# A 3x3 convolution with residual: one image at a time on the full 128x128 array, with row pairs packed on chip

## The chip, the cores and the metric

The kernel runs on one core of one Trainium2 chip. The metric is the device time of one execution in microseconds (us): the median of several executions. Before the change it is 126.52 us, the median of 8 runs between 126.23 and 126.70.

A core has a matrix engine (TensorE, PE in the profile), a vector engine (VectorE, DVE), a scalar engine (ScalarE, ACT), GpSimd (POOL) and SyncE (SP). PE reads SBUF and writes PSUM; the others compute from SBUF and PSUM or only issue transfers. Transfers between HBM and SBUF run on 16 DMA engines, fed by queues which SP, ACT and POOL issue into.

## The reference

`x` and `residual` are 16 x 64 x 64 x 64 in fp32 (images, channels, rows, columns), `weight` is 64 x 64 x 3 x 3. With zero padding of one pixel:

```python
for kh in range(k):
    for kw in range(k):
        output[b, co] += weight[co, ci, kh, kw] * x_pad[b, ci, kh:kh+h, kw:kw+w]
return (output + residual).astype(np.float32)
```

for all images b, output channels co and input channels ci. `x`, `residual` and the output are 16.78 MB each.

## The kernel before

**Tiling.** Two images make a pair: 2 x 64 channels fill the 128 partitions, with one image's 4,096 pixels along each partition. There are 8 pairs. Every pair has its own buffer for x (`xt`, bf16) and its own for the residual (`ro`, fp32), so no load waits for a buffer.

**Loads.** ACT issues the load of the weights (L52). POOL issues the eight x loads (L54), 2 MB each in HBM, cast to bf16 by the DMA; between the first and the rest it makes an identity matrix. SP issues the eight residual loads (L58), 2 MB each. SP also issues the stores (L106), after all residual loads.

**Weights.** VectorE duplicates the weights (L61), PE transposes the nine taps (L67), and VectorE casts the result into `wl` (L70): on partitions 0 to 63 and again on 64 to 127, nine 64 x 64 matrices.

**Convolution.** For a pair, the loop at L79 goes over four chunks of 2 x 8 rows. A chunk has two PSUM tiles of one bank (512 columns). Each of nine taps takes four matmuls of K = 64, M = 64 (L91), one for each 64 x 64 quarter of the array: two images (`half`) times two groups of rows (`swap`). In the second PSUM tile the two images stand exchanged, so that all four quarters are in use. Each matmul has its own weight load. A pair takes 4 x 9 x 4 = 144 matmuls, the kernel 1,152.

**Adding and storing.** VectorE adds the first PSUM tile to the residual in place with one instruction over 128 partitions (L100), and the second with two over 64 partitions each (L105). When a pair's four chunks are done, SP stores it (L106).

**Order.** The loops are written out in full, each engine takes its instructions from the tile framework's schedule, and the framework puts in all waits. [...] up to four chunks can be in work.

Of the kernel before, what the change touches and what calls it, by code (L numbers as in the profile page):

```python
# [1 line left out]

# [5 lines left out]

FP32 = mybir.dt.float32
BF16 = mybir.dt.bfloat16  # L10
ADD = mybir.AluOpType.add


@with_exitstack
def kernel(
    ctx: ExitStack,
    tc: tile.TileContext,
    x: bass.AP,
    weight: bass.AP,
    residual: bass.AP,  # L20
    out: bass.AP,
):
    nc = tc.nc

    B, C, H, W = x.shape
    CO = weight.shape[0]
    K = weight.shape[2]
    assert C == 64 and CO == 64 and K == 3 and H == 64 and W == 64 and B == 16

    NPIX = H * W  # L30
    NPAIR = B // 2
    ROWS = 8
    CHUNK = ROWS * W
    NCHUNK = NPIX // CHUNK

    TAPS = [(1, 1), (1, 0), (1, 2), (0, 1), (0, 0), (0, 2), (2, 1), (2, 0), (2, 2)]

    res_bc = residual.rearrange("b c h w -> (b c) (h w)")
    out_bc = out.rearrange("b c h w -> (b c) (h w)")
    x_bc = x.rearrange("b c h w -> (b c) (h w)")  # L40
    w_flat = weight.rearrange("co ci kh kw -> co (ci kh kw)")

    pool = ctx.enter_context(tc.tile_pool(name="pool", bufs=1))
    psum = ctx.enter_context(tc.tile_pool(name="psum", bufs=8, space=bass.MemoryType.PSUM))


    wdup = pool.tile([64, 2, 576], FP32)
    ident = pool.tile([64, 64], FP32)
    ro = [pool.tile([128, NPIX], FP32, name=f"ro{p}") for p in range(NPAIR)]
    xt = [pool.tile([128, NPIX], BF16, name=f"xt{p}") for p in range(NPAIR)]  # L50

    nc.scalar.dma_start(out=wdup[:, 0, :], in_=w_flat[:, :])  # L52
    for p in range(NPAIR):
        nc.gpsimd.dma_start(out=xt[p][:, :], in_=x_bc[128 * p : 128 * p + 128, :])  # L54
        if p == 0:
            make_identity(nc, ident[:, :])
    for p in range(NPAIR):
        nc.sync.dma_start(out=ro[p][:, :], in_=res_bc[128 * p : 128 * p + 128, :])  # L58


    nc.vector.tensor_copy(out=wdup[:, 1, :], in_=wdup[:, 0, :])  # L61
    wl = pool.tile([128, 9, 64], BF16)
    wdup3 = wdup.rearrange("p d (ci t) -> p (d ci) t", t=9)
    for t0, n in ((0, 8), (8, 1)):
        tp = psum.tile([128, CHUNK], FP32, name="ps")
        for t in range(t0, t0 + n):
            nc.tensor.transpose(  # L67
                out=tp[:, 64 * (t - t0) : 64 * (t - t0) + 64], in_=wdup3[:, :, t], identity=ident[:, :]
            )
        nc.vector.tensor_copy(  # L70
            out=wl[:, t0 : t0 + n, :], in_=tp[:, 0 : 64 * n].rearrange("p (t c) -> p t c", c=64)
        )

    for p in range(NPAIR):
        x3 = xt[p].rearrange("p (h w) -> p h w", w=W)
        o = ro[p]
        for c in range(0, NCHUNK, 2):  # L79
            ps = [psum.tile([128, CHUNK], FP32, name="ps") for _ in range(2)]  # L80
            ps3 = [t.rearrange("p (h w) -> p h w", w=W) for t in ps]
            for i, (kh, kw) in enumerate(TAPS):
                xlo, xhi = max(0, 1 - kw), min(W, W + 1 - kw)
                for swap in range(2):
                    r0 = ROWS * (c + swap)
                    ylo = max(0, 1 - kh - r0)
                    yhi = min(ROWS, H + 1 - kh - r0)
                    for half in range(2):
                        hp = slice(64 * half, 64 * half + 64)
                        to = 64 * (half ^ swap)  # L90
                        nc.tensor.matmul(  # L91
                            out=ps3[swap][to : to + 64, ylo:yhi, xlo:xhi],
                            lhsT=wl[hp, 3 * kh + kw, :],
                            rhs=x3[hp, r0 + ylo + kh - 1 : r0 + yhi + kh - 1, xlo + kw - 1 : xhi + kw - 1],
                            start=i == 0,
                            stop=i == len(TAPS) - 1,
                            skip_group_check=True,
                        )
            sl = slice(CHUNK * c, CHUNK * (c + 1))
            nc.vector.tensor_tensor(out=o[:, sl], in0=ps[0][:, :], in1=o[:, sl], op=ADD)  # L100
            sl = slice(CHUNK * (c + 1), CHUNK * (c + 2))
            for half in range(2):
                hp = slice(64 * half, 64 * half + 64)
                fr = 64 - 64 * half
                nc.vector.tensor_tensor(out=o[hp, sl], in0=ps[1][fr : fr + 64, :], in1=o[hp, sl], op=ADD)  # L105
        nc.sync.dma_start(out=out_bc[128 * p : 128 * p + 128, :], in_=o[:, :])  # L106


# [1 line left out]
_INS = ['x', 'weight', 'residual']  # L110
_OUTS = [((16, 64, 64, 64), 'float32')]


# [23 lines left out]
```

## Time and profile before

| | before |
|---|---|
| median of 8 runs | 126.52 us |
| the profiled execution | 126.68 us |
| its span, first to last instruction | 124.9 us |
| PE busy, matmuls | 66.5 us (53%), 1,161 |
| VectorE busy, instructions | 67.5 us (54%), 99 |
| ACT busy | 0 |
| moved by DMA | 404 GB/s over the span |
| add over 128 x 512 (L100), mean | 692 ns, x32 |
| add over 64 x 512 (L105), mean | 688 ns, x64 |
| copy of the weights (L61), 64 x 576 fp32 | 453 ns |

The span is what the profile can see; the execution's time has 1.8 us more around it. A PE that is shown as busy is not necessarily at its peak, since matmuls overlap: a single one is shown as 384 ns long, [...]. Durations come from one profiled execution, and the other runs lie within 0.2% of the median.

In the page's picture of the span in 40 slices, DMA stands at 9 tenths or more from slice 2 to slice 38, and PE and VectorE are at work from slice 4 to slice 31.

### The profile page before, as it was taken

To read this page: it belongs to the slowest core of one execution; us is meant where nothing else is said; L and a number is where in the kernel's file an instruction comes from. 1 tells how busy PE (TensorE), PEld (TensorE's weight loads), DVE (VectorE), ACT (ScalarE), POOL (GpSimd) and SP (SyncE) were. 2 spreads that over 40 slices of the span, in tenths; PEclk is the share of its full clock that TensorE was granted. 3 is DMA by queue.
4 is the path that set the end of the run, shared out by engine and by line. 5 is a ranking of instruction groups with operands and counts; after the bars stand their busy time and mean duration, and the time that the engine had idled before them with its cause. 6 is when DMAs were issued, how large, how long until landed. Compare 5 with 4: busy or idle time off the path is not lost.

```text
span 124.9 us, 2518 instructions
## 1 busy us (share of the span) xinstructions
PE 66.5 (53%) x1161; PEld 55.3 (44%) x1161; DVE 67.5 (54%) x99; POOL 4.9 (4%) x14
## 2 busy tenths in 40 slices
PE   0003079979949949949967976985990000000000
PEld 0003049948928928927946954963980000000000
DVE  0001204998996996995995995997898000000000
POOL 6900000000000000000000000000000000000000
PEclk9999999999999999999999999999998555555555
DMA  4999999999999999999999999999999999999970
GB/s 100 370 328 299 352 310 296 338 333 299 304 341 315 315 344 307 328 336 296 302 336 331 307 336 333 304 317 420 425 430 420 451 430 425 430 420 436 430 325 10
DMA packets 3547, 42.25 MB, mean 338 GB/s; under 512 B 401, under 2 KB 401, under 8 KB 465
## 3 DMA queue, kind: packets, MB, share of 16 engines
q1 hardware_dynamic: 2304, 33.56, 64.2%
q0 software_dynamic: 1152, 8.39, 32.1%
q8 instruction: 9, 0.15, 0.4%
q10 hardware_dynamic: 80, 0.15, 0.3%
q14 instruction: 2, 0.01, 0.0%
HBM read 33.70 MB, written 16.78 MB: 404 GB/s over the span
## 4 chain that ended last, share of the span: by engine, by line
DMA 35%; PE 27%; DVE 6%; another core or an unknown queue 6%; POOL 1%; issue 1%; DVEq 1%; POOLq 0%
DMA xt<-in_x_dram 35%; PE ps L91 27%; DVE ro L105 4%; DVE ro L100 2%; POOL xt L54 1%; DVEq L132 1%; POOL ident masks.py:199 0%; POOL ident masks.py:197 0%; POOLq masks.py:199 0%; POOLq L121 0%
## 5 line engine op out<-in xcount | busy, mean ns | idle before, releaser
L91 PE MATMUL ps<-xt,wl 64*64 64x504 bf16 (+3 forms) x1152 | 65.2, 384 | 15.8 <-DMA xt<-in_x_dram 15.8
L91 PEld LDWEIGHTS <-wl 64*64 64x64 bf16 x1152 | 54.2, 110 | 26.5 <-DMA xt<-in_x_dram 15.1
L105 DVE TENSOR_TENSOR ro<-ps,ro 64x512 f32<-64x512 f32 x64 | 44.1, 688 | 1.3
L100 DVE TENSOR_TENSOR ro<-ps,ro 128x512 f32<-128x512 f32 x32 | 22.1, 692 | 15.3 <-PE ps L91 14.6
L67 PE MATMUL ps<-ident,wdup 64*128 64x64 f32 x9 | 1.3, 320 | 11.5 <-DVE wdup L61 11.5
L61 DVE COPY wdup<-wdup 64x576 f32<-64x576 f32 x1 | 0.5, 453 | 10.9 <-DMA wdup<-in_weight_dram 10.9
L67 PEld LDWEIGHTS ps<-ident,wdup 64*128 64x128 f32 x9 | 1.1, 205 | 11.5 <-issue 11.5
L54 POOL DMA_DIRECT2D xt<-in_x_dram x8 | 4.4, 583 | 0.8 <-POOLq L121 0.8
L70 DVE CAST wl<-ps 128x512 bf16<-128x512 f32 (+1 forms) x2 | 0.8, 454 | 1.3 <-PE ps L67 1.3
masks.py:199 POOL TENSOR_SCALAR_AFFINE_SELECT ident<-ident 64x64 f32<-64x64 f32 x1 | 0.3, 271 | 0.1
masks.py:197 POOL MEMSET ident<- 64x64 f32 x1 | 0.2, 175 | 0.0
L121 POOL MEMSET const-float32-0.0<- 128x1 f32 x1 | 0.1, 104 | 0.2 <-issue 0.2
L121 POOL MEMSET const-bfloat16-1.0<- 128x1 bf16 x1 | 0.1, 107 | 0.0
L121 POOL MEMSET const-uint8-127<- 128x1 uint8 x1 | 0.1, 107 | 0.0
L121 POOL MEMSET const-float32-1.0<- 128x1 f32 x1 | 0.1, 104 | 0.0
## 6 DMA issues: line engine op xcount, KB each, us to landing
ro<-in_residual_dram SPq DMA_DIRECT2D x8, 2048.0 KB, 44.0
out_dram<-ro SPq DMA_DIRECT2D x8, 2048.0 KB, 44.5
xt<-in_x_dram POOLq DMA_DIRECT2D x8, 1024.0 KB, 47.9
wdup<-in_weight_dram ACTq DMA_DIRECT2D x1, 144.0 KB, 10.2
```

The lines of the kernel that those rows point to most:

```text
L54: nc.gpsimd.dma_start(out=xt[p][:, :], in_=x_bc[128 * p : 128 * p + 128, :])
L61: nc.vector.tensor_copy(out=wdup[:, 1, :], in_=wdup[:, 0, :])
L67: nc.tensor.transpose(out=tp[:, 64 * (t - t0) : 64 * (t - t0) + 64], in_=wdup3[:, :, t], identity=ident[:, :])
L70: nc.vector.tensor_copy(out=wl[:, t0 : t0 + n, :], in_=tp[:, 0 : 64 * n].rearrange("p (t c) -> p t c", c=64))
L91: nc.tensor.matmul(out=ps3[swap][to : to + 64, ylo:yhi, xlo:xhi], lhsT=wl[hp, 3 * kh + kw, :], rhs=x3[hp, r0 + ylo + kh - 1 : r0 + yhi + k ...
L100: nc.vector.tensor_tensor(out=o[:, sl], in0=ps[0][:, :], in1=o[:, sl], op=ADD)
L105: nc.vector.tensor_tensor(out=o[hp, sl], in0=ps[1][fr : fr + 64, :], in1=o[hp, sl], op=ADD)
L121: nc = _bacc.Bacc("TRN2", target_bir_lowering=False, num_devices=1)
L132: with _tile.TileContext(nc) as tc:
```

## The change

Images are now convolved one at a time, each on the full array. The 64 rows of an image are grouped in row pairs: in a new bf16 buffer `xp`, partitions 64 to 127 hold the even rows (row 2j in slot j), and partitions 0 to 63 hold the odd rows one slot later (row 2j-1 in slot j), with zero rows at the ends. So slot j has rows 2j-1 and 2j under each other, and slot j+1 has rows 2j+1 and 2j+2: all four rows which output rows 2j and 2j+1 need. One matmul of K = 128 (two input rows x 64 channels), M = 128 (two output rows x 64 channels) on slots j (d = 0) and one on slots j+1 (d = 1), for each of three horizontal taps, give two output rows: six matmuls per bank of 8 row pairs, 24 per image, 384 in all. Of the eight 64 x 64 blocks in the two weight matrices of a horizontal tap, two are zero.

- `pack(n)` fills `xp` for image n: VectorE copies the even rows, ACT the odd rows. There are four `xp` buffers. x itself has five buffers (`xr`) in place of eight; after the second image of a pair is packed, POOL loads the pair five further on.
- `convolve(n)` uses a PSUM tile of four banks, and there are two such tiles.
- `add(n)` is two VectorE adds of 64 x 2,048, one for the even and one for the odd output rows, with rows of 64 columns at a step of two rows in the residual buffer. After a pair's second image SP stores the pair.
- The weights' start has the same copy and nine transposes, then six casts into the new layout, and memsets for zero rows and zero blocks.
- `tc.manual_schedule()` makes every engine run in the written order: convolve(n), pack(n+2), add(n).

```diff
-    xt = [pool.tile([128, NPIX], BF16, name=f"xt{p}") for p in range(NPAIR)]
+    psum = ctx.enter_context(tc.tile_pool(name="psum", bufs=2, space=bass.MemoryType.PSUM))
+    xr = [pool.tile([128, NPIX], BF16, name=f"xr{i}") for i in range(NXR)]
+    xp = [pool.tile([128, J + 1, W], BF16, name=f"xp{i}") for i in range(4)]
+    wl = pool.tile([128, 2, 3, 2, 64], BF16)
...
+    def pack(n):
+        p, im = divmod(n, 2)
+        hp = slice(64 * im, 64 * im + 64)
+        x4 = xr[p % NXR].rearrange("q (j two w) -> q j two w", two=2, w=W)
+        t = xp[n % 4]
+        nc.vector.tensor_copy(out=t[64:128, 0:J, :], in_=x4[hp, :, 0, :])
+        nc.scalar.copy(out=t[0:64, 1 : J + 1, :], in_=x4[hp, :, 1, :])
+        if im == 1 and p + NXR < NPAIR:
+            load_x(p + NXR)
+
+    def convolve(n):
+        t = xp[n % 4]
+        ps = psum.tile([128, NCHUNK, JC, W], FP32, name="ps")
+        order = [(1, 0), (1, 1), (0, 0), (0, 1), (2, 0), (2, 1)]
+        for i, (kw, d) in enumerate(order):
+            xlo, xhi = max(0, 1 - kw), min(W, W + 1 - kw)
+            for c in range(NCHUNK):
+                j0 = JC * c
+                nc.tensor.matmul(
+                    out=ps[:, c, :, xlo:xhi],
+                    lhsT=wl[:, d, kw, :, :].rearrange("q r c -> q (r c)"),
+                    rhs=t[:, j0 + d : j0 + d + JC, xlo + kw - 1 : xhi + kw - 1],
...
+    def add(n, ps):
+        p, im = divmod(n, 2)
+        hp = slice(64 * im, 64 * im + 64)
+        o4 = ro[p].rearrange("q (j two w) -> q j two w", two=2, w=W)
+        psj = ps.rearrange("q c j w -> q (c j) w")
+        for par in range(2):
+            nc.vector.tensor_tensor(
+                out=o4[hp, :, par, :], in0=psj[64 * par : 64 * par + 64, :, :], in1=o4[hp, :, par, :], op=ADD
             )
+        if im == 1:
+            nc.sync.dma_start(out=out_bc[128 * p : 128 * p + 128, :], in_=ro[p][:, :])
...
+    with tc.manual_schedule():
+        nc.scalar.dma_start(out=wdup[:, 0, :], in_=w_flat[:, :])
+        load_x(0)
+        make_identity(nc, ident[:, :])
+        for p in range(1, NXR):
+            load_x(p)
+        for p in range(NPAIR):
+            load_ro(p)
...
+        for t in xp:
+            nc.vector.memset(t[0:64, 0, :], 0.0)
+            nc.vector.memset(t[64:128, J, :], 0.0)
+        nc.vector.memset(wl[0:64, 0, :, 1, :], 0.0)
+        nc.vector.memset(wl[64:128, 1, :, 0, :], 0.0)
...
+        for half, d, par, kh in (
+            (0, 0, 0, 0),
+            (1, 0, 0, 1),
+            (1, 0, 1, 0),
+            (0, 1, 0, 2),
+            (0, 1, 1, 1),
+            (1, 1, 1, 2),
+        ):
+            hp = slice(64 * half, 64 * half + 64)
+            nc.vector.tensor_copy(out=wl[hp, d, :, par, :], in_=tpf[hp, 3 * kh : 3 * kh + 3, :])
+
+        pack(0)
+        pack(1)
+        for n in range(B):
+            ps = convolve(n)
+            if n + 2 < B:
+                pack(n + 2)
+            add(n, ps)
```

More of the change, by code (lines that the diff above doesn't have):

```diff
@@ L31 @@
     NPAIR = B // 2
[L32 to L36, printed above, removed]
+    J = H // 2
+    JC = 8
+    NCHUNK = J // JC
+    NXR = 5
     res_bc = residual.rearrange("b c h w -> (b c) (h w)")
@@ L43 @@
     pool = ctx.enter_context(tc.tile_pool(name="pool", bufs=1))
-    psum = ctx.enter_context(tc.tile_pool(name="psum", bufs=8, space=bass.MemoryType.PSUM))
+    psum = ctx.enter_context(tc.tile_pool(name="psum", bufs=2, space=bass.MemoryType.PSUM))
     wdup = pool.tile([64, 2, 576], FP32)
@@ L49 @@
     ro = [pool.tile([128, NPIX], FP32, name=f"ro{p}") for p in range(NPAIR)]
-    xt = [pool.tile([128, NPIX], BF16, name=f"xt{p}") for p in range(NPAIR)]
[L52 to L57, printed above, removed]
-        nc.sync.dma_start(out=ro[p][:, :], in_=res_bc[128 * p : 128 * p + 128, :])
@@ L61 @@
[L61 to L68, printed above, removed]
-            )
-        nc.vector.tensor_copy(
-            out=wl[:, t0 : t0 + n, :], in_=tp[:, 0 : 64 * n].rearrange("p (t c) -> p t c", c=64)
-        )
@@ L76 @@
[L76 to L106, printed above, removed]
@@ new lines, with load_x, load_ro @@
+    xr = [pool.tile([128, NPIX], BF16, name=f"xr{i}") for i in range(NXR)]
+    xp = [pool.tile([128, J + 1, W], BF16, name=f"xp{i}") for i in range(4)]
+    wl = pool.tile([128, 2, 3, 2, 64], BF16)
+    def load_x(p):
+        nc.gpsimd.dma_start(out=xr[p % NXR][:, :], in_=x_bc[128 * p : 128 * p + 128, :])
+    def load_ro(p):
+        nc.sync.dma_start(out=ro[p][:, :], in_=res_bc[128 * p : 128 * p + 128, :])
+    def pack(n):
[7 more added lines that the diff above has]
+            load_x(p + NXR)
@@ new lines, in convolve @@
+    def convolve(n):
[10 more added lines that the diff above has]
+                    rhs=t[:, j0 + d : j0 + d + JC, xlo + kw - 1 : xhi + kw - 1],
+                    start=i == 0,
+                    stop=i == len(order) - 1,
+                    skip_group_check=True,
+                )
+        return ps
@@ new lines @@
+    with tc.manual_schedule():
[11 more added lines that the diff above has]
+        nc.vector.memset(wl[64:128, 1, :, 0, :], 0.0)
+        nc.vector.tensor_copy(out=wdup[:, 1, :], in_=wdup[:, 0, :])
+        wdup3 = wdup.rearrange("p d (ci t) -> p (d ci) t", t=9)
+        tp = psum.tile([128, NCHUNK, JC, W], FP32, name="ps")
+        for t in range(9):
+            nc.tensor.transpose(out=tp[:, t // 8, t % 8, :], in_=wdup3[:, :, t], identity=ident[:, :])
+        tpf = tp.rearrange("p c j w -> p (c j) w")
+        for half, d, par, kh in (
[15 more added lines that the diff above has]
+            add(n, ps)
```

## The prediction

> **What bounds the kernel now.** I read the page's DMA queues first, then stretches of the span by engine, then PE's and VectorE's timelines, and last SP's waits and single issues. The queues (packets, MB, share of 16 engines):
>
> ```profile
> q1 hardware_dynamic: 2304, 33.56, 64.2%
> q0 software_dynamic: 1152, 8.39, 32.1%
> q8 instruction: 9, 0.15, 0.4%
> ...
> HBM read 33.70 MB, written 16.78 MB: 404 GB/s over the span
> ```
>
> q1 (residual in, output out) and q0 (x, cast to bf16 on the way) fill 96.3% of 16 engines over the whole span: 50.5 MB, whatever the compute engines do. When they are full is seen in the stretches (PE, weight loads, DVE, POOL, clock, DMA share, GB/s):
>
> ```profile
> 0.00:10.00 10.00, 0.00 (x0) 0.00 (x0) 0.00 (x0) 4.90 (x14) 1.00 0.84 270
> ...
> 70.00:80.00 10.00, 8.05 (x154) 6.64 (x150) 8.43 (x13) 0.00 (x0) 1.00 1.02 319
> ...
> 90.00:95.00 5.00, 3.75 (x72) 3.03 (x64) 4.89 (x9) 0.00 (x0) 1.00 1.01 426
> ...
> 110.00:120.00 10.00, 0.00 (x0) 0.00 (x0) 0.00 (x0) 0.00 (x0) 0.50 1.02 436
> ```
>
> The DMA share is 1.0 to 120 us; compute is gone long before. PE's timeline, then VectorE's last line:
>
> ```profile
> 16.44 9.97 PE L91 MATMUL ps<-xt,wl 64*64 64x512 bf16 x144 [3.68 <-DMA xt<-in_x_dram]
> 27.32 7.89 PE L91 MATMUL ps<-xt,wl 64*64 64x512 bf16 x144 [0.91 <-DMA xt<-in_x_dram]
> 36.85 7.89 PE L91 MATMUL ps<-xt,wl 64*64 64x512 bf16 x144 [1.63 <-DMA xt<-in_x_dram]
> ...
> 85.85 7.89 PE L91 MATMUL ps<-xt,wl 64*64 64x512 bf16 x144 [1.90 <-DMA xt<-in_x_dram]
> ```
>
> ```profile
> 94.97 1.39 DVE L105 TENSOR_TENSOR ro<-ps,ro 64x512 f32<-64x512 f32 x2
> ```
>
> A pair of images arrives every 9.8 us, PE needs 7.89 us for it and waits about 1.9 us for the next. The last add ends at 96.36 us, 28.5 us before the end. What fills that gap are the stores: SP's waits, and the issue of the last store (in the stretch from 96 to 98 us), which takes 27.2 us to land:
>
> ```profile
> SPq L106 <- DVE ro L105: 81.9, 8, 17.4
> SPq L132 <- DMA out_dram<-ro: 26.8, 1, 26.8
> ```
>
> ```profile
> out_dram<-ro SPq DMA_DIRECT2D x1, 2048.0 KB, 27.2
> ```
>
> The first store is issued at 28.98 us and takes 59.3 us, the seventh (86.8) 32.0 us: landings at 88.3, 118.8 and 123.6. All stores lie behind the eight residual loads [...] and run from about 84 us back to back, 4.8 us each. So compute has slack, and its size decides this case. Packets of the last store flow until about 122 us; at 4.8 to 4.9 us for it, its turn comes at 117. SP's first issue is at 0.74 us and its first packets lie in the stretch 1 to 2 us, so I allow 1.3 us: the last add may end at **115.7 us** without moving the end; now it ends 19 us earlier.
>
> [...] 144 matmuls in 7.89 us are (7.89 - 0.38) / 35.75 = 210 ns a round of four, 501 columns on average, though each tile gets new weights every round. No row shows the full array. [...]
>
> **The change part by part.**
>
> *DMA.* The same 50.5 MB in the same queues, and SP's order stays: eight residual loads, then the stores. On POOL five x loads are issued at the start; loads 5, 6, 7 wait for the packs of pairs 0, 1, 2, at about 20, 33 and 44 us. Behind each waiting load stand only later x loads. Five loads are 5 x 9.8 = 49 us of queue, so q0 doesn't run dry. Cost 0; without that cover it would be lost DMA time one for one.
>
> *Instruction fetch.* 1152 matmuls with as many weight loads become 16 x 24 = 384 with theirs: 1,536 of 2,518 instructions go, and VectorE, ACT and SP change by tens. q8 moves 0.15 MB / 2,518 = 60 B each. About 60% of 0.4% of 124.9 us is **-0.3 us** on full DMA engines; nothing if the fetches sit on engines that end early, up to -1.2 us if they sit on the one that ends last (packets thin out from 120 us, and a straggler runs to 122.7).
>
> *Weights at the start.* Ten memsets lie under VectorE's 10.94 us wait for the weights. Six casts of 192 columns replace two: by the rows of 215 ns (64) and 692 ns (512), about 350 ns each, 2.1 us from 12.8, ending at 15.0. x lands at 16.4 and must be packed first. Hidden, with over 3 us to spare; an ACT table load in front costs 1.3 us there and is hidden too.
>
> *Packing.* One VectorE copy per image (64 x 2,048 bf16): [...] 0.73 us. [...] ACT's copy of the other half, [...] 1.89 us, lies beside PE, one per image; twice that would still hide.
>
> *Adds.* Two per image, 64 x 2,048: [...] **4.65 us per image**, 74.4 us for 16 (now 66.2). Full-width adds disappear, so VectorE does more, not less.
>
> *Matmuls.* 24 per image, 507 columns on average: 212 ns, period 5.09 us, 5.26 to the last end; 81.4 us for 16 against 8 x 7.89 = 63.1 now. [...]
>
> *Order and waits.* VectorE runs pack(n+2), then add(n). Behind the pack of a new pair's first image stands an add that is ready: add(0) waits until pair 1 lands, 27.3 us. PSUM holds two images, so convolve(n+2) waits for add(n).
> Chain: x at 16.4, ACT to 18.4, convolve(0) and (1) with the 2.1 us of slow start seen in 9.97 against 7.89, to about 31. VectorE starts at 27.35: pack(2), add(0) to 32.8, pack(3), add(1) to 38.1. From there a period is 0.73 + 4.65 = 5.38 us on VectorE and 5.09 on PE. Between add(n) and add(n+2) VectorE has 6.11 us of other work, and the convolution needs 5.26 plus two handovers, so VectorE sets the pace, 10.8 us a pair against 9.8 for arrival. Last add: 27.35 + 14 x 0.73 + 74.4 = **112.0 us**, 113.5 with 0.1 us of handover per image. It uses up 16 us of slack and stays 2 to 4 under 115.7. Pair 6 is ready at 102 for a turn at 112, pair 0 at 38 for 84.
>
> **Sum.** Slack used, 0; fetch, -0.3: the profiled execution's 126.68 us (124.9 span, 1.8 around it) gives 126.4. It lies 0.16 over the median of 126.52, so **126.2 us**.
>
> **The rivals.**
> 1. [...] (two strided sides of different row counts in memory, no such row in the trace). [...] It decides from a pack of 1.0 us on. This is the slower side. [...]
> 2. *Full-array weight loads not hidden.* PE sets the pace from 32.9 us: 14 periods + 4.9. The border is a period of 5.56 us, 232 ns a matmul. [...]
> 3. *Small stalls in the written order*, 0.4 us or more per image, put the last add at 118.4 or later, 2.7 late: **128.9 us**. For it: PE and VectorE alternate with only 0.7 us of play.
> 4. *The straggler engine was late because of fetches*: the whole -1.2 us: **125.3 us**. For it: 0.4% of 16 engines are 8 us of one engine. Against it: nothing shows which engines fetch.
> That the change doesn't do what it says would show as another matmul count; its code leaves no doubt.
>
> **How the numbers follow.** My forecast, with DMA as the wall, gets 0.56, rival 4 0.10; rival 1 0.12, rival 2 0.08, rival 3 0.14. A measurement of this kernel can tell about 0.2% (0.25 us) from no change. The forecast's own span is 125.9 to 126.9, [...] I split it 0.26 faster, 0.25 same, 0.05 slower. Faster: 0.26 + 0.10 = 0.36. Slower: 0.05 + 0.34 = 0.39. Same: 0.25. Range: 125.3 takes in rival 4, 130.5 takes in rivals 1 [...] and 3; left out are rival 2 [...].
>
> **What would show it.** Right: DMA share 1.0 to 120 us, last add at 111 to 115 us, packs near 0.7 us, matmul spacing near 212 ns, last store landing 10 to 13 us after its issue, q8 with about 4 packets. Wrong: an empty DMA stretch ahead of the last store, packs over 1 us, PE rounds over 232 ns, or a gap in q0 before pair 5.

## The result, and the profile after

| | before | after |
|---|---|---|
| median | 126.57 us (32 runs) | 125.40 us (11 runs, 125.04 to 125.79) |
| ratio, 95% interval | | 0.9907 (0.9895 to 0.9920) |
| the profiled execution | 126.68 us | 125.42 us |
| its span | 124.9 us | 123.6 us |
| PE busy | 66.5 us | 88.2 us |
| VectorE busy | 67.5 us | 87.6 us |
| last add ends | 96.4 us | 111.1 us |
| instructions | 2,518 | 1,002 |

The changed kernel is 1.2 us or 0.9% faster, although PE and VectorE each work 20 us longer or more, and the last add ends 15 us later. The DMA queues of the changed kernel:

```profile
q1 hardware_dynamic: 2304, 33.56, 64.9%
q0 software_dynamic: 1152, 8.39, 32.4%
...
q8 instruction: 3, 0.05, 0.1%
q14 instruction: 1, 0.01, 0.0%
HBM read 33.70 MB, written 16.78 MB: 408 GB/s over the span
```

q1 and q0 move the same packets and bytes as before. In microseconds their share is the same too: 97.3% of 123.6 is 120.3 us, 96.3% of 124.9 was also 120.3. What has changed are the queues that bring instructions: q8 has 3 packets for 9, and q14 one small packet for two. (q14 is out as a cause: two of the kernels below have one packet there and 9 on q8, and don't gain.) Stretches of the changed kernel (PE, weight loads, DVE, ACT, POOL, clock, DMA share, GB/s):

```profile
90.00:95.00 5.00, 5.00 (x24) 2.12 (x23) 4.94 (x4) 0.00 (x0) 0.00 (x0) 1.00 1.04 439
...
110.00:120.00 10.00, 0.00 (x0) 0.00 (x0) 1.14 (x1) 0.00 (x0) 0.00 (x0) 0.53 1.02 436
```

The DMA share is again 1.0 up to 120 us. PE and VectorE, which had pauses of almost 2 us per pair, are now busy throughout (5.00 and 4.94 of 5 us), and nothing comes of it, since neither sets the end: the last add ends at 111.1 us, the last DMA packet at 122.0. What differs is the last three microseconds. First the kernel before, whose rows have no ACT column, then the changed one:

```profile
120.00:121.00 1.00, 0.00 (x0) 0.00 (x0) 0.00 (x0) 0.00 (x0) 0.50 0.73 311
121.00:122.00 1.00, 0.00 (x0) 0.00 (x0) 0.00 (x0) 0.00 (x0) 0.50 0.20 82
122.00:123.00 1.00, 0.00 (x0) 0.00 (x0) 0.00 (x0) 0.00 (x0) 0.50 0.08 33
```

```profile
120.00:121.00 1.00, 0.00 (x0) 0.00 (x0) 0.00 (x0) 0.00 (x0) 0.00 (x0) 0.50 0.46 197
121.00:122.00 1.00, 0.00 (x0) 0.00 (x0) 0.00 (x0) 0.00 (x0) 0.00 (x0) 0.50 0.12 49
122.00:123.00 1.00, 0.00 (x0) 0.00 (x0) 0.00 (x0) 0.00 (x0) 0.00 (x0) 0.50 0.00 0
```

A share of 0.08 of 16 engines over 1 us is 1.3 us of one engine. Before, the work of about one engine still ran between 122 and 123 us; after, nothing does. The mean over the engines moved little: the shares of these three rows sum to 1.01 us before and 0.58 after, 0.4 us less. The last engine moved by more than 1 us: by the times of the single packets in the traces, the last one ends at 123.2 us before and at 122.0 after, and the last store can't have landed earlier.

The chain of waits doesn't help here: it ends with the last add in both kernels, and says "PE 60%" of the changed one. The time is set by what runs beside it. In all eleven traces of this document the execution's time is the end of the last DMA packet plus 3.4 to 3.6 us. The last add and the last store of the changed kernel, from VectorE's timeline and from the store's issue (stretch 111 to 113 us):

```profile
106.55 4.59 DVE L94 TENSOR_TENSOR ro<-ps,ro 64x2048 f32<-64x2048 f32 x2 [0.74 <-PE ps L78]
```

```profile
out_dram<-ro SPq DMA_DIRECT2D x1, 2048.0 KB, 11.2
```

The store issued at about 111.5 us takes 11.2 us to land, while one alone took 6.3 us (shown below). By these two it still has about 5 us of queue before it. In the packet times of the kernel before, q1 carries the eight residual loads one after another, 9.8 us apart, and behind them, from 79.5 us on, the eight stores, from the second on 4.9 to 5.0 us apart.

### The profile page after: what moved, and what is told of

Same layout as the page of the kernel before. It is cut to its first block, busy times and chain, and to the rows that moved or that the text cites. A ratio compares the mean times of both kernels' runs of the same rounds, so it can differ in the third digit from the quotient of the medians.

```text
span 123.6 us, 1002 instructions
## 1 busy us (share of the span) xinstructions
PE 88.2 (71%) x393; PEld 38.1 (31%) x393; DVE 87.6 (71%) x65; ACT 31.6 (26%) x17; POOL 4.9 (4%) x14
## 3 DMA queue, kind: packets, MB, share of 16 engines
q1 hardware_dynamic: 2304, 33.56, 64.9%
## 4 chain that ended last, share of the span: by engine, by line
PE 60%; DMA 19%; DVE 6%; DVEq 2%; issue 1%; POOL 1%; POOLq 0%
PE ps L78 60%; DMA xr<-in_x_dram 19%; DVE ro L94 6%; DVEq L166 2%; POOL xr L54 1%; POOL ident masks.py:199 0%; POOL ident masks.py:197 0%; DVE xp L65 0%; POOLq masks.py:199 0%; POOLq L155 0%
## 5 line engine op out<-in xcount | busy, mean ns | idle before, releaser
L78 PE MATMUL ps<-xp,wl 128*128 128x504 bf16 (+1 forms) x384 | 87.0, 385 | 6.7 <-ACT xp L66 5.6
L94 DVE TENSOR_TENSOR ro<-ps,ro 64x2048 f32<-64x2048 f32 x32 | 73.2, 2289 | 1.5 <-PE ps L78 0.9
L78 PEld LDWEIGHTS <-wl 128*128 128x128 bf16 x384 | 37.0, 99 | 56.4 <-issue 10.9
L66 ACT COPY xp<-xr 64x2048 bf16<-64x2048 bf16 x16 | 30.4, 1897 | 56.8 <-DMA xr<-in_x_dram 56.6
L65 DVE COPY xp<-xr 64x2048 bf16<-64x2048 bf16 x16 | 11.0, 689 | 10.5 <-DMA xr<-in_x_dram 10.0
L54 POOL DMA_DIRECT2D xr<-in_x_dram x8 | 4.4, 555 | 38.8 <-DVE xp L65 21.9
L132 DVE CAST wl<-ps 64x192 bf16<-64x192 f32 x6 | 2.0, 352 | 1.5 <-PE ps L121 1.4
L111 DVE MEMSET xp<- 64x32 uint32 x4 | 0.3, 85 | 0.9 <-PEq L155 0.8
L112 DVE MEMSET xp<- 64x32 uint32 x4 | 0.3, 85 | 0.2
```

The source lines that it names most:

```text
L54: nc.gpsimd.dma_start(out=xr[p % NXR][:, :], in_=x_bc[128 * p : 128 * p + 128, :])
L65: nc.vector.tensor_copy(out=t[64:128, 0:J, :], in_=x4[hp, :, 0, :])
L66: nc.scalar.copy(out=t[0:64, 1 : J + 1, :], in_=x4[hp, :, 1, :])
L78: nc.tensor.matmul(out=ps[:, c, :, xlo:xhi], lhsT=wl[:, d, kw, :, :].rearrange("q r c -> q (r c)"), rhs=t[:, j0 + d : j0 + d + JC, xlo + k ...
L94: nc.vector.tensor_tensor(out=o4[hp, :, par, :], in0=psj[64 * par : 64 * par + 64, :, :], in1=o4[hp, :, par, :], op=ADD)
L111: nc.vector.memset(t[0:64, 0, :], 0.0)
```

## Experiments

My theory after the result: DMA sets the end, compute has slack, and the gain is the smaller number of instruction fetches. The rivals: the five x buffers with their gated loads, or the later issue of the stores, treat the DMA engines better; or the slack isn't what I took it for. Ratios are to the kernel before, run beside each experiment (126.6 to 126.7 us).

**Fewer matmuls in the kernel before.** Six of nine taps are left out, so 384 matmuls and as many weight loads remain.

```diff
-    TAPS = [(1, 1), (1, 0), (1, 2), (0, 1), (0, 0), (0, 2), (2, 1), (2, 0), (2, 2)]
+    TAPS = [(1, 1), (1, 0), (1, 2)]
```

> The kernel before with three of the nine taps (kh = 1 only; six taps are left out of the sum), so 384 matmuls and weight loads instead of 1,152; transfers, adds, buffers and stores as before. Theory (instruction fetch takes DMA time, and the changed kernel gains by fetching less): 3 fetch packets in place of 9, 125.4 us, like the changed kernel. Rival (the gain comes from the five x buffers with gated loads, or from stores being queued later): 126.5 us, as before.

Measured: 125.28 us, ratio 0.9889 (0.9858 to 0.9920). It is the same gain as the whole change brings, without row pairs, x buffers or a new order. Its q8 and its last stretches:

```profile
q8 instruction: 3, 0.05, 0.1%
```

```profile
120.00:121.00 1.00, 0.00 (x0) 0.00 (x0) 0.00 (x0) 0.00 (x0) 0.50 0.31 131
121.00:122.00 1.00, 0.00 (x0) 0.00 (x0) 0.00 (x0) 0.00 (x0) 0.50 0.08 33
122.00:123.00 1.00, 0.00 (x0) 0.00 (x0) 0.00 (x0) 0.00 (x0) 0.50 0.00 0
```

Three packets, and nothing left from 122 us on, as in the changed kernel. Its stores are issued from 26.5 us on and its last add ends at 95.7 us, both earlier than in the changed kernel, so a later issue of the stores isn't what gains.

**Five x buffers in the kernel before.**

```diff
-    xt = [pool.tile([128, NPIX], BF16, name=f"xt{p}") for p in range(NPAIR)]
+    NXR = 5
+    xr = [pool.tile([128, NPIX], BF16, name=f"xt{i}") for i in range(NXR)]
+    xt = [xr[p % NXR] for p in range(NPAIR)]
...
-    for p in range(NPAIR):
+    for p in range(NXR):
         nc.gpsimd.dma_start(out=xt[p][:, :], in_=x_bc[128 * p : 128 * p + 128, :])
...
         nc.sync.dma_start(out=out_bc[128 * p : 128 * p + 128, :], in_=o[:, :])
+        q = p + NXR
+        if q < NPAIR:
+            nc.gpsimd.dma_start(out=xt[q][:, :], in_=x_bc[128 * q : 128 * q + 128, :])
```

> The kernel before with five x buffers in place of eight; x loads 5 to 7 are issued when the pair five earlier is convolved. All instructions as before. Theory (instruction fetch): 126.5 us, 9 fetch packets. Rival (gated x loads help the DMA engines): 125.4 us.

Measured: 126.73 us, ratio 1.0006 (0.9986 to 1.0026). Gated loads neither gain nor cost anything that shows.

**The number of matmuls of before in the changed kernel.** Every matmul is cut into three by rows; PE streams the same columns.

```diff
+                for lo, hi in ((0, 3), (3, 6), (6, 8)):
-                    out=ps[:, c, :, xlo:xhi],
+                    out=ps[:, c, lo:hi, xlo:xhi],
...
-                    rhs=t[:, j0 + d : j0 + d + JC, xlo + kw - 1 : xhi + kw - 1],
-                    start=i == 0,
+                    rhs=t[:, j0 + d + lo : j0 + d + hi, xlo + kw - 1 : xhi + kw - 1],
+                    start=i == 0 and lo == 0,
```

> The changed kernel with every matmul cut into three by rows (3, 3 and 2 of 8): 1,152 matmuls and weight loads with the same columns in sum, the number of before. Theory (instruction fetch): 9 fetch packets again and 126.5 us, if PE stays near 5.3 us an image so that the last add ends before 115.7 us; if short matmuls slow PE to 5.8 us an image, the last add ends near 118 us and the time is 128 or more. Rival (gated loads or later stores make the gain): 125.4 us.

Measured: 126.51 us, ratio 0.9987 (0.9972 to 1.0001). The gain is gone, while compute is on time: the last add ends at 111.0 us, against 111.1 in the changed kernel. Its q8 and its last stretch:

```profile
q8 instruction: 9, 0.15, 0.4%
```

```profile
122.00:123.00 1.00, 0.00 (x0) 0.00 (x0) 0.00 (x0) 0.00 (x0) 0.00 (x0) 0.50 0.04 16
```

With 9 packets there is again an engine at work after 122 us. Taking packets away from the old kernel and giving them back to the new one moves the time by the same 1.1 to 1.3 us in both directions.

**How the cost depends on the number.** In the kernel before with one tap (eight are left out) and in the changed kernel with every matmul cut in two (rows 0 to 3 and 4 to 7) the count goes to 1 and 6.

> The kernel before with one tap of nine (kh = kw = 1; eight taps are left out of the sum): 128 matmuls and weight loads. Theory (instruction fetch on full DMA engines): 1 fetch packet; against three taps 2 packets fewer, 2 x 0.95 us of one engine or 0.1 us as a mean over 16, up to 0.4 us if they sat on the engine that ends last: 124.9 to 125.2 us. Rival (what counts is the matmuls' own traffic or PE's activity): a step as large as that from nine taps to three, a third of it per three taps or 0.4 us, or more.

> The changed kernel with every matmul cut in two by rows: 768 matmuls and weight loads, 6 fetch packets. Theory (instruction fetch): between the changed kernel and its three-way cut, 125.7 to 126.2 us. Rival (the extra time of the three-way cut came from short matmuls or the adds behind them): 125.4 us, as PE has no fewer pauses here.

Measured: 125.29 us for one tap, ratio 0.9894 (0.9876 to 0.9912), a miss by 0.1 us: no step from 3 packets to 1 can be told. Cut in two: 125.48 us, ratio 0.9903 (0.9887 to 0.9920), a miss too. I had put it between the changed kernel and its three-way cut, and it stands with the changed kernel. So the cost isn't proportional, and short matmuls alone don't bring it. The next two kernels were made for the question of where the step lies: 8 packets (three pieces for the first four of six weight matrices, two for the rest) and 10 (three and four pieces). The edits are shown against the three-way cut.

```diff
-                for lo, hi in ((0, 3), (3, 6), (6, 8)):
+                for lo, hi in ((0, 3), (3, 6), (6, 8)) if i < 4 else ((0, 4), (4, 8)):
```

```diff
-                for lo, hi in ((0, 3), (3, 6), (6, 8)):
+                for lo, hi in ((0, 3), (3, 6), (6, 8)) if i < 4 else ((0, 2), (2, 4), (4, 6), (6, 8)):
```

> The changed kernel with two thirds of the matmuls cut in three and one third cut in two: 1,024 matmuls and weight loads, 8 fetch packets. So far 1, 3 and 6 packets gave 125.3, 125.4 and 125.5 us, 9 gave 126.5. Theory (a packet delays only the DMA engine that it runs on, each of the first eight another one, and the ninth falls on an engine that has had one): 125.5 us, with the last engine's last packet near 122.1 us. Rival (the cost grows with the number of packets, or short matmuls do it): two thirds of the way from 6 to 9 packets, 126.1 us or more.

> The changed kernel with two thirds of the matmuls cut in three and one third in four: 1,280 matmuls and weight loads, 10 fetch packets. Theory (two engines then have two packets each, the last one is no later than with nine): 126.5 us, as with nine, if PE still keeps up and the last add ends before 115.7 us. Rival (cost by number): 126.8 us.

Measured: 125.55 us for 8, ratio 0.9923 (0.9905 to 0.9940), and 126.65 us for 10, ratio 1.0000 (0.9985 to 1.0015). The first is what the theory said (125.5 us, the rival 126.1 or more). The second lies midway between theory (126.5) and rival (126.8) and doesn't tell them apart. All counts together:

| matmuls and weight loads | q8 packets | kernel | ratio to before |
|---|---|---|---|
| 256 | 1 | before, one tap | 0.9894 |
| 768 | 3 | before, three taps | 0.9889 |
| 768 | 3 | changed | 0.9907 |
| 1,536 | 6 | changed, cut in two | 0.9903 |
| 2,048 | 8 | changed, cut in three and two | 0.9923 |
| 2,304 | 9 | changed, cut in three | 0.9987 |
| 2,304 | 9 | before, five x buffers | 1.0006 |
| 2,560 | 10 | changed, cut in three and four | 1.0000 |

There is one packet for each 256 matmuls and weight loads, and one step, between 8 and 9 packets. The last stretches of the kernels with 8 and with 10 packets:

```profile
121.00:122.00 1.00, 0.00 (x0) 0.00 (x0) 0.00 (x0) 0.00 (x0) 0.00 (x0) 0.50 0.27 115
122.00:123.00 1.00, 0.00 (x0) 0.00 (x0) 0.00 (x0) 0.00 (x0) 0.00 (x0) 0.50 0.00 0
```

```profile
121.00:122.00 1.00, 0.00 (x0) 0.00 (x0) 0.00 (x0) 0.00 (x0) 0.00 (x0) 0.50 0.35 147
122.00:123.00 1.00, 0.00 (x0) 0.00 (x0) 0.00 (x0) 0.00 (x0) 0.00 (x0) 0.50 0.08 33
```

With 8, more engines are late than in the changed kernel (0.27 against 0.12 between 121 and 122 us), but nothing is left after 122; with 10, the stretch after 122 us is filled as it was before. This would fit if each of eight engines takes one fetch packet and the ninth packet falls on an engine that has had one, which is an inference from these times and counts. The profile doesn't say on which engine a packet ran, but the packet times in the traces tell part of it. From 90 us on only stores are left beside the fetches, and each packet on an engine starts within 0.02 us of the end of the one before, so that the packets can be joined into 16 chains. In the kernel before and in the one with five x buffers, the ninth fetch packet (at 92.7 and 93.0 us) stands in the chain that ends last, at 123.2 and 122.9 us; the next chain ends at 121.9 in both. With ten packets, the ninth stands in the chain that ends last (123.1 us) and the tenth in the one ahead of it (122.9); the third from the end is done at 122.4. In the three-way cut the links aren't unique.

So it is shown that the step is tied to the count, not to which kernel, order or buffers stand around it, and that in these three traces the ninth packet runs on the engine that ends last. That this engine had one of the first eight remains inferred, since the links are less certain while x is still being loaded. Matmuls and packets were never varied apart; it is the chains that speak against the matmuls themselves as the cause.

**The size of the slack.** VectorE makes its pack copy twice.

```diff
-        nc.vector.tensor_copy(out=t[64:128, 0:J, :], in_=x4[hp, :, 0, :])
+        for _ in range(2):
+            nc.vector.tensor_copy(out=t[64:128, 0:J, :], in_=x4[hp, :, 0, :])
```

> The changed kernel with VectorE's pack copy made twice, so that VectorE needs 0.72 us more per image. Theory (slack up to 115.7 us for the last add): 14 x 0.72 = 10 us later, last add at 121.2 us, 5.5 us over the slack, time 125.4 + 5.5 = 130.9 us. Rival (no slack, the adds set the end already): 125.4 + 10 = 135.5 us. Second rival (the last store has far more room): 125.4 us.

Measured: 130.32 us, ratio 1.0288 (1.0256 to 1.0320). Its last adds and, between them and the store, the DMA engines:

```profile
116.22 4.59 DVE L95 TENSOR_TENSOR ro<-ps,ro 64x2048 f32<-64x2048 f32 x2 [0.91 <-PE ps L79]
```

```profile
115.00:116.00 1.00, 1.00 (x6) 0.32 (x4) 0.31 (x1) 0.00 (x0) 0.00 (x0) 1.00 1.08 459
116.00:117.00 1.00, 0.18 (x1) 0.00 (x0) 0.78 (x1) 0.00 (x0) 0.00 (x0) 1.00 0.20 82
117.00:118.00 1.00, 0.00 (x0) 0.00 (x0) 1.00 (x1) 0.00 (x0) 0.00 (x0) 1.00 0.00 0
118.00:119.00 1.00, 0.00 (x0) 0.00 (x0) 0.99 (x2) 0.00 (x0) 0.00 (x0) 0.91 0.00 0
119.00:120.00 1.00, 0.00 (x0) 0.00 (x0) 1.00 (x1) 0.00 (x0) 0.00 (x0) 0.50 0.00 0
120.00:121.00 1.00, 0.00 (x0) 0.00 (x0) 0.81 (x1) 0.00 (x0) 0.00 (x0) 0.50 0.00 0
121.00:122.00 1.00, 0.00 (x0) 0.00 (x0) 0.00 (x0) 0.00 (x0) 0.00 (x0) 0.50 0.61 262
```

The last add ends at 120.81 us. From 117 to 121 us the DMA share is 0: all other stores are done and the last is not yet issued. It lands 6.3 us after its issue, with nothing queued before it. The time rises by 4.9 us for 9.7 us of later compute. If every microsecond past the edge counts in full, as the empty stretch suggests, the edge lies at 120.8 - 4.9 = 115.9 us.

**Feeding the queues faster at the start.** Between 2 and 4 us the engines are not full. The first residual load goes to ACT's queue.

```diff
+        nc.scalar.dma_start(out=ro[0][:, :], in_=res_bc[0:128, :])
-        for p in range(NPAIR):
+        for p in range(1, NPAIR):
             load_ro(p)
```

> The changed kernel with the first residual load issued from ACT's queue, behind the weights, and SP starting with the second. Between 2 and 4 us the DMA share is only 0.5 to 0.8, about 0.6 us of all engines lost. Theory (SP alone doesn't feed the engines fast enough at the start): up to 0.6 us gained, 124.8 us. Rival (the gap is something else, such as the first packets' latency): 125.4 us. With three queues x arrives later at first; by the slack of 4 us to the last add that costs nothing.

Measured: 125.63 us, ratio 0.9925 (0.9902 to 0.9949): no gain, and the gap stays. The changed kernel first, then this one:

```profile
2.00:3.00 1.00, 0.00 (x0) 0.00 (x0) 0.14 (x2) 0.59 (x1) 0.93 (x4) 1.00 0.83 147
3.00:4.00 1.00, 0.00 (x0) 0.00 (x0) 0.00 (x0) 0.00 (x0) 1.00 (x3) 1.00 0.56 229
```

```profile
2.00:3.00 1.00, 0.00 (x0) 0.00 (x0) 0.14 (x1) 1.00 (x1) 0.93 (x4) 1.00 0.55 131
3.00:4.00 1.00, 0.00 (x0) 0.00 (x0) 0.00 (x0) 0.22 (x1) 1.00 (x3) 1.00 0.61 246
```

A second issuing queue doesn't close the gap, so that SP alone feeds too slowly isn't borne out; what makes the gap stays open. x came later here, the first pair at 19.6 us against 16.5 in the changed kernel and the second at 31.2 against 26.3, so the whole chain ran later and the last add ended at 116.0 us. The expectation had allowed for that by its slack of 4 us; it took all of it and reached the edge. No version that beats the changed kernel came out of these runs: q1 and q0 alone need 120.3 us of full engines, and what they leave is the start and the last landing.

## Why the prediction was right or wrong

The wall was right, and so were the steps that decide whether compute reaches it. The predicted end of the last add, 112.0 to 113.5 us, against 111.1 measured, comes from terms that the changed kernel's groups bear out one by one (busy us, mean ns):

```profile
L94 DVE TENSOR_TENSOR ro<-ps,ro 64x2048 f32<-64x2048 f32 x32 | 73.2, 2289 | 1.5 <-PE ps L78 0.9
...
L66 ACT COPY xp<-xr 64x2048 bf16<-64x2048 bf16 x16 | 30.4, 1897 | 56.8 <-DMA xr<-in_x_dram 56.6
L65 DVE COPY xp<-xr 64x2048 bf16<-64x2048 bf16 x16 | 11.0, 689 | 10.5 <-DMA xr<-in_x_dram 10.0
...
L132 DVE CAST wl<-ps 64x192 bf16<-64x192 f32 x6 | 2.0, 352 | 1.5 <-PE ps L121 1.4
```

- *Adds* were put at 4.65 us an image and took 4.62 up to the start of what follows, two of 2,289 ns; the *pack* was put at 0.73 us and took 0.72 to 0.73, 689 ns of it the copy itself; ACT's copy, put at 1.89 us, took 1.90; a *cast* at 350 ns took 352; the table load in front of ACT's copies at 1.3 us took 1.28. The cast was worked out from rows of the profile of before. The others were the author's estimates, and no row of before has their sizes; the changed kernel's rows bear them out to 2%, with operands of strided rows. Rival 1, a pack of 1.0 us or more, is out.
- *Matmuls* were put at 212 ns. With PE waiting before each image, as in the kernel with the double copy, 24 of them take 5.35 us from first start to last end, (5.35 - 0.38) / 23 = 216 ns. Each has its own weight load, 99 ns on average in the changed kernel, and at 216 ns, 4 over the 212 worked out and 16 under the border of 232, no such load is added: weight loads are hidden on the full array as well here, and rival 2 is out.
- *Order and waits*: a period of 5.38 us was worked out, and in the changed kernel adds with a pack between them start 5.32 us apart (91.10 and 96.42 us). VectorE waits for PE only 0.9 us in all, at the end. Rival 3 is out. The second pair landed at 26.3 us, 1 us ahead of the assumed 27.3; that is most of what the last add came early.
- *Slack*: 115.7 us predicted, 115.9 worked out from the double copy.
- *DMA order and gated loads*: cost 0, as the five buffers in the kernel before and the DMA share of 1.0 up to 120 us in the changed one show.

The step that was off is the size of *Instruction fetch*: -0.3 us in the forecast, -1.17 between the medians. The count was near (4 packets predicted, 3 measured), and the mean over 16 engines is indeed about 0.4 us. But the end isn't set by the mean. It is set by the engine that ends last, and there the old kernel's ninth packet ran. In the chains one fetch delays its engine by 1.3 us (0.93 + 0.99 - 0.61, worked out in the last section), enough for the whole difference. The prediction had this as rival 4, with 0.10 and 125.3 us, and that is what happened. The evidence for it stood in the profile of before: at 122 to 123 us a share of 0.08, about one engine alone, with everything else done. I took the mean because no view names the engines; the straggler itself was there to be priced. It was also read a little short: the prediction lets it run to 122.7 us, but its last packet starts at 122.6 and ends at 123.2.

So the time of 126.2 us was 0.8 us too high, and 125.4 lies below the span of 125.9 to 126.9 that the forecast gave itself. It lies inside the stated range, at its lower end, only because the range had been drawn to take in rival 4. The change did what its words say to the engines, but what it gains has nothing to do with their work. It gains because one matmul of K = M = 128 replaces three of 64 x 64 in the instruction stream.

## What to carry to other kernels

When the DMA engines are full from end to end, as here (a share of 1.0 up to 120 us), price a change by what it does to the DMA engines, and look for transfers nobody wrote: here one fetch packet of 16 KB came by the same engines for each 256 matmuls and weight loads. Look at the last microseconds by share of 16 engines; if about one engine runs alone, as here (a share of 0.08 between 122 and 123 us), the end is a question of balance. The cost of the fetch packets came in one step here, from 8 to 9, and not in proportion. And work out the latest moment at which the last producer may finish without delaying its store; up to there more compute is free (15 us of it here), beyond it the time rises (by 4.9 us here, for an add that ended at 120.8).

## What the runs showed of the hardware that was not expected

- A fetch packet of 16 KB occupies a DMA engine for about 0.9 us (0.4% of 16 x 124.9 us, by 9; 0.88 to 0.97 us by the packet times of the kernel before), where a data packet of the same size takes about 0.6 us (a 2 MB store is 8 rows of 16 KB per engine in 4.8 to 4.9 us). While only stores run, the data packet behind a fetch takes about 1.0 us, so one fetch delays its engine by about 1.3 us (0.93 + 0.99 - 0.61).
- From 8 to 9 fetch packets the time goes up by 0.6 to 0.8% (ratios 0.9923 and 0.9987 to 1.0006), from 1 to 8 by at most 0.35%, from 9 to 10 not measurably.
- Weight loads of 128 x 128 stayed hidden behind short matmuls too. With 1,280 matmuls, 152 columns on average, each with its own weight load (shown as 99 ns long on average), PE's 16 images took 88.4 us with waits, 69 ns a matmul, and the last add ended at 111.3 us, 0.2 us later than with 384 matmuls.
